# In-place Ln for the last four tiles, a split first load and a new order of the last Exps in a prefix log-sum-exp scan

## Chip, core and metric

The kernel runs on one core of one Trainium2 chip. The metric is the time of one execution on the device in microseconds (us). The kernel before took 1259.39 us, the median of five runs (1258.61 to 1263.86).

## The reference

The input `x` is 8 x 4096 x 2048 in float32. For each of the 8 sequences and each of the 2048 columns the output is the running log-sum-exp along the 4096 time steps:

```
out[:, 0, :] = x[:, 0, :]
mx = maximum(out[:, t-1, :], x[:, t, :])
out[:, t, :] = mx + log(exp(out[:, t-1, :] - mx) + exp(x[:, t, :] - mx))
```

The kernel computes the same quantity as Ln of a prefix sum of Exp. Input and output are 268 MB each, and each is moved once.

## The kernel before

**Tiles.** A tile is 512 time steps of one sequence by all 2048 columns. It lies in SBUF as 128 partitions x 4 rows x 2048 columns: partition p holds the steps 4p to 4p+3. It is 4 MB. There are 64 tiles (`NT`), numbered 0 to 63, eight to a sequence (`NBLK`). Work on a tile is done in two halves of 1024 columns, h = 0 and h = 1.

**Buffers.** Four load buffers `ti` (`NI`), two store buffers `to` (`NO`), two PSUM tiles `ps`. Tile n uses `ti[n % 4]`, `to[n % 2]` and `ps[n % 2]`.

**Steps of a tile**, all ordered by semaphores that are set by hand:

- SP issues the load into `ti` (L111). A load of tile n+4 waits for the `freed` that ScalarE sends when the Ln of tile n is done.
- ScalarE takes Exp in place in `ti`, one instruction for each half (`exp`, L127).
- VectorE adds the four rows up within each partition, three additions of 128 x 1024 for each half (`local`, L232). It takes both halves before it goes on.
- TensorE multiplies the last row by a triangle of ones, which gives every partition the sum of those before it (`triangle`, L208).
- VectorE adds that to all four rows, one 128 x 4096 addition for each half (`join`, L241).
- TensorE carries the tile's last sum over to the next tile's PSUM (`carry`, L197). At the end of a sequence this is only an event. It then raises `carried`.
- ScalarE takes Ln from `ti` into `to`, for each half (`ln`, L132). Half 0 waits until the store before last, which used the same `to`, has landed (`stored`). Each half waits for its `carried`.
- ScalarE waits for both Ln's (`logs`), raises `freed` and issues the store (`store`, L140).

**Order on ScalarE.** Its stream is written out by hand. Two Exps of tile 0 stand first. A loop of 15 turns over four tiles each then has, for n from 1 to 60: Exp of n (both halves), Ln of n-1 (both halves), `freed`, store of n-1. What stands after the loop treats the Exps of tiles 61 to 63 and the Ln's and stores of tiles 60 to 63. For the last pair the order is: Ln of 62 half 0, store of that half, Exp of 63 (both halves), Ln of 62 half 1 and its store, then Ln and store of tile 63 by halves. A step on ScalarE that waits holds up all that stands behind it.

**Queues.** Loads and stores run in two queues, one of SP's and one of ScalarE's, that share the core's 16 DMA engines. The landing of a transfer is complete when all of its engines have reported.

Of the kernel before, what the change touches and what calls it, by code (L numbers as in the profile page):

```python
# [9 lines left out]
def kernel(  # L10
# [2 lines left out]
    x: bass.AP,  # L13
    out: bass.AP,
):

# [13 lines left out]
    ACT = mybir.ActivationFunctionType  # L32
# [46 lines left out]
    with tc.tile_critical():  # L79
        def sems(name, n):  # L80
            return [nc.alloc_semaphore(f"{name}{i}") for i in range(n)]

        ones, shaped, freed, logs = (sems(s, 1)[0] for s in ("ones", "shaped", "freed", "logs"))

        loaded, stored = sems("loaded", NI), sems("stored", NO)
        exps, chain, sums, ahead, joined, carried = (
# [3 lines left out]
        with nc.Block() as block:  # L90

            @block.gpsimd
            def _(g):
                g.memset(before[:], 1.0).then_inc(ones, 1)  # L94
                g.memset(last[:], 1.0).then_inc(ones, 1)  # L95
                g.wait_ge(ones, 2)

                g.affine_select(  # L98
                    out=before[:], in_=before[:], compare_op=mybir.AluOpType.is_ge, fill=0.0,
                    base=-1, pattern=[[1, P]], channel_multiplier=-1,  # L100
                ).then_inc(shaped, 1)

                g.affine_select(  # L103
                    out=last[:], in_=last[:], compare_op=mybir.AluOpType.is_ge, fill=0.0,
                    base=-(P - 1), pattern=[[0, P]], channel_multiplier=1,
                ).then_inc(shaped, 1)

            @block.sync
            def _(sp):
                def load(src, n):  # L110
                    sp.dma_start(out=ti[n][:], in_=src).then_inc(loaded[n], 16)  # L111

                for n in range(NI):
                    load(x_v[n], n)
                with sp.Fori(1, NT // NI) as j:
                    for n in range(NI):
                        sp.wait_ge(freed, n + 1)
                        load(x_v[bass.ds(j * NI + n, 1)][0], n)
                    take(sp, freed, NI)

            @block.scalar
            def _(act):
                def exp(n, h):
                    t = ti[n % NI]
                    if h == 0:
                        take(act, loaded[n % NI], 16)
                    act.activation(t[:, :, half(h)], t[:, :, half(h)], ACT.Exp).then_inc(exps[h], 1)  # L127

                def ln(n, h, turn):
                    if h == 0:  # L130
                        take(act, stored[n % NO], 16)
                    act.activation(  # L132
                        to[n % NO][:, :, half(h)], ti[n % NI][:, :, half(h)], ACT.Ln
                    )._wait_ge(carried[h], turn + 1).then_inc(logs, 1)

                def store(n, dst, h=None, landing=16):
                    t = to[n % NO][:]
                    if h is not None:
                        t, dst = t[:, :, half(h)], dst[:, :, half(h)]
                    act.dma_start(out=dst, in_=t).then_inc(stored[n % NO], landing)  # L140

                def done(turn):

                    event(act, [(logs, 2 * turn + 2)], [(freed, "sem-add-imm", 1)])

                def settle(turns):
                    take(act, carried[0], turns)
                    take(act, carried[1], turns)
                    take(act, logs, 2 * turns)

                for n in range(NO):
                    act.sem_inc(stored[n], 16)
                exp(0, 0)
                exp(0, 1)
                turns = (NT - 2) // NI
                with act.Fori(0, turns) as j:
                    for n in range(1, NI + 1):
                        exp(n, 0)
                        exp(n, 1)
                        ln(n - 1, 0, n - 1)  # L160
                        ln(n - 1, 1, n - 1)
                        done(n - 1)
                        store(n - 1, o_v[bass.ds(j * NI + (n - 1), 1)][0])
                    settle(NI)
                rest = range(1 + turns * NI, NT)
                for turn, n in enumerate(rest):
                    final = n == NT - 1
                    if final:

                        ln(n - 1, 0, turn)  # L170
                        act.wait_ge(logs, 2 * turn + 1)
                        store(n - 1, o_v[n - 1], 0)
                    exp(n, 0)
                    exp(n, 1)
                    if not final:
                        ln(n - 1, 0, turn)
                    ln(n - 1, 1, turn)
                    act.wait_ge(logs, 2 * turn + 2)
                    store(n - 1, o_v[n - 1], 1 if final else None)
                for h in range(2):  # L180
                    ln(NT - 1, h, len(rest))
                    act.wait_ge(logs, 2 * len(rest) + h + 1)
                    store(NT - 1, o_v[NT - 1], h)
                settle(len(rest) + 1)
                for n in (NT - 2, NT - 1):
                    take(act, stored[n % NO], 32)

            @block.tensor
            def _(pe):
                def carry(k, h):  # L190

                    if k == NBLK - 1:
                        event(pe, [(joined[h], k + 1)], [(carried[h], "sem-add-imm", 1)])
                        return
                    for c in range(2 * h, 2 * h + 2):
                        sl = slice(c * FD, (c + 1) * FD)
                        m = pe.matmul(  # L197
                            ps[(k + 1) % 2][:, sl], last[:], ti[k % NI][:, R - 1, sl],
                            start=True, stop=False, skip_group_check=True,
                        )  # L200
                        if c == 2 * h:
                            m._wait_ge(joined[h], k + 1)
                    m.then_inc(carried[h], 1)

                def triangle(k, h):
                    for c in range(2 * h, 2 * h + 2):
                        sl = slice(c * FD, (c + 1) * FD)
                        m = pe.matmul(  # L208
                            ps[k % 2][:, sl], before[:], ti[k % NI][:, R - 1, sl],
                            start=k == 0, stop=True, skip_group_check=True,  # L210
                        )
                        if c == 2 * h:
                            m._wait_ge(sums[h], k + 1)
                    m.then_inc(ahead[h], 1)

                pe.wait_ge(shaped, 2)
                with pe.Fori(0, B):
                    for k in range(NBLK):
                        for h in range(2):
                            triangle(k, h)  # L220
                        for h in range(2):
                            carry(k, h)
                    for h in range(2):
                        take(pe, sums[h], NBLK)
                        take(pe, joined[h], NBLK)

            @block.vector
            def _(dve):
                def local(n, h):
                    t = ti[n]  # L230
                    for r in range(1, R):
                        a = dve.tensor_add(t[:, r, half(h)], t[:, r - 1, half(h)], t[:, r, half(h)])  # L232
                        if r == 1:
                            a._wait_ge(exps[h], n + 1)
                        else:
                            a._wait_ge(chain[h], (R - 2) * n + r - 1)
                        a.then_inc(*((chain[h], 1) if r < R - 1 else (sums[h], 1)))

                def join(n, h):
                    t = ti[n]  # L240
                    dve.tensor_add(  # L241
                        t[:, :, half(h)], t[:, :, half(h)],
                        ps[n % 2][:, half(h)].unsqueeze(1).to_broadcast([P, R, HALF]),
                    )._wait_ge(ahead[h], n + 1).then_inc(joined[h], 1)

                with dve.Fori(0, NT // NI):  # L246
                    for n in range(NI):
                        for h in range(2):
                            local(n, h)
                        for h in range(2):  # L250
                            join(n, h)
                    for h in range(2):
                        take(dve, exps[h], NI)
                        take(dve, chain[h], (R - 2) * NI)
                        take(dve, ahead[h], NI)
# [30 lines left out]
```

The softmax here doesn't subtract the row's maximum and nothing guards it: scores larger than these inputs give would overflow.

## Time and profile before

| what | value |
|---|---|
| median of five runs | 1259.39 us |
| the profiled execution: its time / its span | 1258.78 us / 1257.1 us |
| DMA | 268.44 MB read and 268.44 MB written, mean 427 GB/s over the span |
| VectorE busy | 1023.3 us, 81% |
| ScalarE busy | 913.4 us, 73% |
| TensorE busy | 653.6 us, 52%, mean granted clock 0.783 |
| load, 4096 KB | 64 times, median 31.2 us from issue to landing |
| store, 4096 KB / 2048 KB | 62 / 4 times, median 31.4 / 7.3 us |

Times inside an execution are counted from the start of the span. The span ends some 1.7 us short of the execution's time. Where a row of the profile says "idle before", the engine had nothing to do for so long ahead of that row; the name after the arrow is what ended it. "ACTq L61" means that the engine was held by its own sequencer at a semaphore event, the `take` of line 77, whose instruction is built at line 61.

### The profile page before, as it was taken

To read this page: it belongs to the slowest core of one execution; us is meant where nothing else is said; L and a number is where in the kernel's file an instruction comes from. 1 tells how busy PE (TensorE), PEld (TensorE's weight loads), DVE (VectorE), ACT (ScalarE), POOL (GpSimd) and SP (SyncE) were. 2 spreads that over 40 slices of the span, in tenths; PEclk is the share of its full clock that TensorE was granted. 3 is DMA by queue.
4 is the path that set the end of the run, shared out by engine and by line. 5 is a ranking of instruction groups with operands and counts; after the bars stand their busy time and mean duration, and the time that the engine had idled before them with its cause. 6 is when DMAs were issued, how large, how long until landed. Compare 5 with 4: busy or idle time off the path is not lost. (4 is left out here: it accounts for less than half of the span.)

```text
span 1257.1 us, 3678 instructions
## 1 busy us (share of the span) xinstructions
PE 653.6 (52%) x960; PEld 216.7 (17%) x960; DVE 1023.3 (81%) x512; ACT 913.4 (73%) x257; POOL 1.1 (0%) x8
## 2 busy tenths in 40 slices
PE   2656365553554636555445564555544655455551
PEld 0211121111211211111111111121111211111110
DVE  4999788787887977878778788787887878878865
ACT  5876866777767767677686776866867768677675
POOL 0000000000000000000000000000000000000000
PEclk9897777877778768778687786887768878678776
DMA  9999999999999999999999999999999999999987
GB/s 400 412 433 431 433 432 432 434 431 434 433 434 434 434 434 434 434 433 434 434 434 434 433 434 434 433 433 433 432 433 433 434 433 434 434 433 434 434 381 300
DMA packets 20258, 536.90 MB, mean 427 GB/s; under 512 B 2080, under 2 KB 2080, under 8 KB 4128
## 3 DMA queue, kind: packets, MB, share of 16 engines
q10 hardware_dynamic: 11040, 268.44, 49.6%
q1 hardware_dynamic: 9216, 268.44, 49.6%
q8 instruction: 1, 0.02, 0.0%
q14 instruction: 1, 0.01, 0.0%
HBM read 268.44 MB, written 268.44 MB: 427 GB/s over the span
## 5 line engine op out<-in xcount | busy, mean ns | idle before, releaser
L132 ACT ACTIVATE to<-ti 128x4096 f32<-128x4096 f32 x128 | 456.4, 3609 | 266.9 <-ACTq L61 257.8
L232 DVE TENSOR_TENSOR ti<-ti 128x1024 f32<-128x1024 f32 x384 | 464.6, 1224 | 211.1 <-ACT ti L127 202.3
L241 DVE TENSOR_TENSOR ti<-ti,ps 128x4096 f32<-128x4096 f32 x128 | 560.0, 4417 | 9.8 <-PE ps L208 9.5
L208 PE MATMUL ps<-ti,before 128*128 128x512 f32 x512 | 384.1, 903 | 350.0 <-DVE ti L232 349.2
L127 ACT ACTIVATE ti<-ti 128x4096 f32<-128x4096 f32 x128 | 455.9, 3609 | 66.9 <-ACTq L61 66.9
L197 PE MATMUL ps<-ti,last 128*128 128x512 f32 x448 | 269.5, 732 | 233.9 <-DVE ti L241 233.9
L208 PEld LDWEIGHTS ps<-ti,before 128*128 128x128 f32 x512 | 130.2, 282 | 619.4 <-DVE ti L232 510.8
L197 PEld LDWEIGHTS ps<-ti,last 128*128 128x128 f32 x448 | 86.4, 214 | 400.6 <-DVE ti L241 334.4
L33 ACT ACT_TABLE_LOAD x1 | 1.3, 1283 | 0.8 <-PEq L270 0.8
L98 POOL TENSOR_SCALAR_AFFINE_SELECT before<-before 128x128 f32<-128x128 f32 x1 | 0.3, 295 | 0.1
L103 POOL TENSOR_SCALAR_AFFINE_SELECT last<-last 128x128 f32<-128x128 f32 x1 | 0.3, 295 | 0.0
L95 POOL MEMSET last<- 128x128 f32 x1 | 0.2, 206 | 0.0
L94 POOL MEMSET before<- 128x128 f32 x1 | 0.2, 205 | 0.5 <-SPq L79 0.5
L270 POOL MEMSET const-bfloat16-1.0<- 128x1 bf16 x1 | 0.1, 102 | 0.0
L270 POOL MEMSET const-uint8-127<- 128x1 uint8 x1 | 0.1, 102 | 0.0
L270 POOL MEMSET const-float32-0.0<- 128x1 f32 x1 | 0.1, 99 | 0.3 <-issue 0.3
L270 POOL MEMSET const-float32-1.0<- 128x1 f32 x1 | 0.1, 99 | 0.0
## 6 DMA issues: line engine op xcount, KB each, us to landing
ti<-in_x_dram SPq DMA_DIRECT2D x64, 4096.0 KB, 31.2
out_dram<-to ACTq DMA_DIRECT2D x62, 4096.0 KB, 31.4
out_dram<-to ACTq DMA_DIRECT2D x4, 2048.0 KB, 7.3
```

Source lines behind the costliest of these rows:

```text
L33: nc.scalar.preload_act_table_set("natural_log_exp_and_others")
L94: g.memset(before[:], 1.0).then_inc(ones, 1)
L95: g.memset(last[:], 1.0).then_inc(ones, 1)
L98: g.affine_select(out=before[:], in_=before[:], compare_op=mybir.AluOpType.is_ge, fill=0.0, base=-1, pattern=[[1, P]], channel_multiplier= ...
L103: g.affine_select(out=last[:], in_=last[:], compare_op=mybir.AluOpType.is_ge, fill=0.0, base=-(P - 1), pattern=[[0, P]], channel_multiplier=1,
L127: act.activation(t[:, :, half(h)], t[:, :, half(h)], ACT.Exp).then_inc(exps[h], 1)
L132: act.activation(to[n % NO][:, :, half(h)], ti[n % NI][:, :, half(h)], ACT.Ln)._wait_ge(carried[h], turn + 1).then_inc(logs, 1)
L197: m = pe.matmul(ps[(k + 1) % 2][:, sl], last[:], ti[k % NI][:, R - 1, sl], start=True, stop=False, skip_group_check=True,)
L208: m = pe.matmul(ps[k % 2][:, sl], before[:], ti[k % NI][:, R - 1, sl], start=k == 0, stop=True, skip_group_check=True,)
L232: a = dve.tensor_add(t[:, r, half(h)], t[:, r - 1, half(h)], t[:, r, half(h)])
L241: dve.tensor_add(t[:, :, half(h)], t[:, :, half(h)], ps[n % 2][:, half(h)].unsqueeze(1).to_broadcast([P, R, HALF]),)._wait_ge(ahead[h], n ...
L270: nc = _bacc.Bacc("TRN2", target_bir_lowering=False, num_devices=1)
```

## The change

The change touches the two ends of the program. The loop over the tiles and the instructions of TensorE, VectorE and GpSimd stay as they are.

- **First tile.** Its load is split in two, rows 0 and 1 and rows 2 and 3 of each partition. ScalarE takes Exp of rows 0 and 1 over all columns in one instruction when the first part has landed (`top`), and then Exp of rows 2 and 3 by halves.
- **Last four tiles (60 to 63).** Ln writes in place in `ti`, so it does not wait for a store of `to`. Their stores read `ti` and raise one semaphore of their own (`final`). No load follows into these buffers.
- **Order.** For the last pair the order becomes: Ln of 62 half 0, Exp of 63 half 0, Ln of 62 half 1, store of 62 in one transfer, Exp of 63 half 1, then Ln and store of 63 by halves as before.

```diff
-                for n in range(NI):
+                sp.dma_start(out=ti[0][:, 0:2, :], in_=x_v[0][:, 0:2, :]).then_inc(top, 16)
+                sp.dma_start(out=ti[0][:, 2:R, :], in_=x_v[0][:, 2:R, :]).then_inc(loaded[0], 16)
+                for n in range(1, NI):
                     load(x_v[n], n)
...
-                def ln(n, h, turn):
-                    if h == 0:
+                def ln(n, h, turn, in_place=False):
+                    if h == 0 and not in_place:
                         take(act, stored[n % NO], 16)
                     act.activation(
-                        to[n % NO][:, :, half(h)], ti[n % NI][:, :, half(h)], ACT.Ln
+                        (ti[n % NI] if in_place else to[n % NO])[:, :, half(h)],
+                        ti[n % NI][:, :, half(h)], ACT.Ln,
                     )._wait_ge(carried[h], turn + 1).then_inc(logs, 1)
...
-                exp(0, 0)
-                exp(0, 1)
+                take(act, top, 16)
+                act.activation(ti[0][:, 0:2, :], ti[0][:, 0:2, :], ACT.Exp)
+                exp(0, 0, slice(2, R))
+                exp(0, 1, slice(2, R))
...
-                rest = range(1 + turns * NI, NT)
-                for turn, n in enumerate(rest):
-                    final = n == NT - 1
-                    if final:
-                        ln(n - 1, 0, turn)
-                        act.wait_ge(logs, 2 * turn + 1)
-                        store(n - 1, o_v[n - 1], 0)
-                    exp(n, 0)
-                    exp(n, 1)
-                    if not final:
-                        ln(n - 1, 0, turn)
-                    ln(n - 1, 1, turn)
-                    act.wait_ge(logs, 2 * turn + 2)
-                    store(n - 1, o_v[n - 1], 1 if final else None)
+                for n in range(first + 1, NT):
+                    up = n - 1
+                    if n < NT - 1:
+                        exp(n, 0)
+                        exp(n, 1)
+                        ln(up, 0, up - first, True)
+                        ln(up, 1, up - first, True)
+                        finals += store(up)
+                    else:
+                        ln(up, 0, up - first, True)
+                        exp(n, 0)
+                        ln(up, 1, up - first, True)
+                        finals += store(up)
+                        exp(n, 1)
                 for h in range(2):
-                    ln(NT - 1, h, len(rest))
-                    act.wait_ge(logs, 2 * len(rest) + h + 1)
-                    store(NT - 1, o_v[NT - 1], h)
+                    ln(NT - 1, h, NT - 1 - first, True)
+                    finals += store(NT - 1, h)
```

More of the change, by code (lines that the diff above doesn't have):

```diff
@@ L81, in sems @@
             return [nc.alloc_semaphore(f"{name}{i}") for i in range(n)]
-        ones, shaped, freed, logs = (sems(s, 1)[0] for s in ("ones", "shaped", "freed", "logs"))
+        ones, shaped, freed, logs, top, final = (
+            sems(s, 1)[0] for s in ("ones", "shaped", "freed", "logs", "top", "final")
+        )
         loaded, stored = sems("loaded", NI), sems("stored", NO)
@@ L122, in _, with exp @@
             def _(act):
-                def exp(n, h):
+                def exp(n, h, rows=slice(0, R)):
                     t = ti[n % NI]
@@ L126, in exp @@
                         take(act, loaded[n % NI], 16)
-                    act.activation(t[:, :, half(h)], t[:, :, half(h)], ACT.Exp).then_inc(exps[h], 1)
-                def ln(n, h, turn):
-                    if h == 0:
+                    act.activation(
+                        t[:, rows, half(h)], t[:, rows, half(h)], ACT.Exp
+                    ).then_inc(exps[h], 1)
+                def ln(n, h, turn, in_place=False):
+                    if h == 0 and not in_place:
                         take(act, stored[n % NO], 16)
                     act.activation(
-                        to[n % NO][:, :, half(h)], ti[n % NI][:, :, half(h)], ACT.Ln
+                        (ti[n % NI] if in_place else to[n % NO])[:, :, half(h)],
+                        ti[n % NI][:, :, half(h)], ACT.Ln,
                     )._wait_ge(carried[h], turn + 1).then_inc(logs, 1)
[L136 to L144, printed above, removed]
                 def settle(turns):
@@ L161, in _ @@
                         ln(n - 1, 1, n - 1)
-                        done(n - 1)
-                        store(n - 1, o_v[bass.ds(j * NI + (n - 1), 1)][0])
+                        event(act, [(logs, 2 * n)], [(freed, "sem-add-imm", 1)])
+                        act.dma_start(
+                            out=o_v[bass.ds(j * NI + (n - 1), 1)][0], in_=to[(n - 1) % NO][:]
+                        ).then_inc(stored[(n - 1) % NO], 16)
                     settle(NI)
-                rest = range(1 + turns * NI, NT)
@@ L180, in _, with store @@
-                for h in range(2):
-                    ln(NT - 1, h, len(rest))
-                    act.wait_ge(logs, 2 * len(rest) + h + 1)
-                    store(NT - 1, o_v[NT - 1], h)
-                settle(len(rest) + 1)
-                for n in (NT - 2, NT - 1):
-                    take(act, stored[n % NO], 32)
+                first = turns * NI
+                finals = 0
+                def store(n, h=None):
+                    cols = slice(0, D) if h is None else half(h)
+                    act.wait_ge(logs, 2 * (n - first) + (2 if h is None else h + 1))
+                    act.dma_start(
+                        out=o_v[n][:, :, cols], in_=ti[n % NI][:, :, cols]
+                    ).then_inc(final, 16)
+                    return 1
@@ L188, in _ @@
+                for h in range(2):
+                    ln(NT - 1, h, NT - 1 - first, True)
+                    finals += store(NT - 1, h)
+                settle(NT - first)
+                for n in range(NO):
+                    take(act, stored[n], 16)
+                take(act, final, 16 * finals)
             @block.tensor
```

## The prediction

> **What bounds the kernel now.** I read the slices of the page first, then the DMA share stretch by stretch at both ends, then ScalarE and VectorE in order of time there. The chain that ended last covers only the last 19 us, so it names the end but not its cause. From the page, a slice being 31.4 us:
>
> ```profile
> GB/s 400 412 433 431 433 432 432 434 431 434 433 434 434 434 434 434 434 433 434 434 434 434 433 434 434 433 433 433 432 433 433 434 433 434 434 433 434 434 381 300
> L132 ACT ACTIVATE to<-ti 128x4096 f32<-128x4096 f32 x128 | 456.4, 3609 | 266.9 <-ACTq L61 257.8
> L127 ACT ACTIVATE ti<-ti 128x4096 f32<-128x4096 f32 x128 | 455.9, 3609 | 66.9 <-ACTq L61 66.9
> ```
>
> From the third to the 38th slice the DMA moves 431 to 434 GB/s. ScalarE's 257.8 us of waiting ahead of Ln is a wait for landed stores. So the middle is bound by transfers, and the change doesn't touch it. Only slices 1, 2, 39 and 40 are lower. The stretches there (columns: stretch, length, busy of PE, PEld, DVE, ACT, POOL, clock, DMA share, GB/s):
>
> ```profile
> 13.00:41.00 28.00, 14.64 (x21) 5.13 (x22) 23.54 (x15) 21.48 (x6) 0.00 (x0) 0.94 1.00 431
> 41.00:44.00 3.00, 1.69 (x4) 0.38 (x2) 3.00 (x1) 2.47 (x1) 0.00 (x0) 1.00 0.79 175
> 44.00:64.00 20.00, 12.59 (x20) 4.09 (x20) 19.64 (x10) 18.88 (x7) 0.00 (x0) 0.83 1.01 436
> 1214.00:1218.00 4.00, 3.55 (x4) 1.18 (x4) 4.00 (x2) 3.62 (x2) 0.00 (x0) 0.57 0.14 57
> ```
>
> There is one hole at 41 to 44 us, worth 3 x (434 - 175) / 434 = 1.8 us, and one at 1214 to 1218 us. After the last, compute sets the pace. The first hole is explained by ScalarE's and VectorE's order in time at the start:
>
> ```profile
> 13.32 7.12 ACT L127 ACTIVATE ti<-ti 128x4096 f32<-128x4096 f32 x2 [11.22 <-ACTq L61]
> 37.11 3.62 ACT L132 ACTIVATE to<-ti 128x4096 f32<-128x4096 f32 x1 [2.41 <-PE ps L197]
> 40.99 0.40 ACTq L140 DMA_DIRECT2D out_dram<-to  x1
> ```
> ```profile
> 16.97 7.40 DVE L232 TENSOR_TENSOR ti<-ti 128x1024 f32<-128x1024 f32 x6 [16.97 <-ACT ti L127]
> ```
>
> The first four loads are through at 42.3 (load 0 lands at 13.2, the others each 9.7 later). The next load and the first store are issued only at 41.0, since Ln of tile 0 ends at 40.7. That Ln hangs on carry and join, and so on VectorE, which starts at 16.97 with the first Exp and is busy without a gap over 0.3 us. A load takes some 1.9 us to flow (issue 1.03, landing 12.2 us on, less 9.7 + the last engine's 0.5).
>
> The end, ScalarE and VectorE:
>
> ```profile
> 1171.64 7.12 ACT L132 ACTIVATE to<-ti 128x4096 f32<-128x4096 f32 x2 [4.47 <-ACTq L61]
> 1179.88 7.12 ACT L127 ACTIVATE ti<-ti 128x4096 f32<-128x4096 f32 x2 [1.12 <-ACTq L61]
> 1191.05 7.12 ACT L132 ACTIVATE to<-ti 128x4096 f32<-128x4096 f32 x2 [4.05 <-ACTq L61]
> 1210.50 7.12 ACT L132 ACTIVATE to<-ti 128x4096 f32<-128x4096 f32 x2 [4.67 <-ACTq L61]
> 1220.05 3.62 ACT L132 ACTIVATE to<-ti 128x4096 f32<-128x4096 f32 x1 [2.43 <-ACTq L61]
> 1224.46 7.12 ACT L127 ACTIVATE ti<-ti 128x4096 f32<-128x4096 f32 x2 [0.79 <-ACTq L61]
> ```
> ```profile
> 1190.95 8.75 DVE L241 TENSOR_TENSOR ti<-ti,ps 128x4096 f32<-128x4096 f32 x2
> 1202.35 7.40 DVE L232 TENSOR_TENSOR ti<-ti 128x1024 f32<-128x1024 f32 x6 [2.65 <-ACT ti L127]
> 1228.11 7.40 DVE L232 TENSOR_TENSOR ti<-ti 128x1024 f32<-128x1024 f32 x6 [9.39 <-ACT ti L127]
> 1235.43 8.75 DVE L241 TENSOR_TENSOR ti<-ti,ps 128x4096 f32<-128x4096 f32 x2
> ```
>
> The Ln's are of tiles 59, 60, 61 and 62 (half 0); the Exps of 61 and 63. Ln of 60, 61 and 62 wait 4.05, 4.67 and 2.43 us for stores 58, 59 and 60 to leave `to`. VectorE gets tile 63 only at 1228.11, after 9.39 us idle. From the end of its local sums (1235.5) on, join, Ln, two half stores and landing fill the 21.6 us to 1257.1.
>
> **What the skill says.** "ScalarE: Activation LUTs", What ACT_TABLE_LOAD costs: an ACTIVATE takes 186 ns + 0.833 ns per element, and neighbours overlap by some 93 ns. The trace agrees: 3598 ns by the formula at 4096 elements, 3609 measured, a pair in 7.12 us. "DMA: Bandwidth & Descriptors", Why a DMA increments its semaphore by 16: a DMA's engines finish independently and only the full count is a landing. The trace agrees: store 60, issued at 1198.2, lands 21.7 us later, at 1219.9, though from 1214 nearly all engines are idle (share 0.14). A straggling engine holds Ln of 62. "TensorE: Matmul & The Clock Gate", Part 1: the array runs at half or full clock by its recent activity, in free-running windows of 3.4 us. The trace agrees: a half tile's carry takes 1.98 us in 48 of 56 tiles and up to 3.68 in the other 8 (half 0).
>
> **The change part by part.** All times are on the clock of the execution before.
>
> *First load and Exp.* The two loads take SP one issue more, 0.4 us, hidden by the 9.7 us of queued transfer. Rows 0 and 1 (2 MB, half of 9.7 us) land near 8.4; their Exp (3.6 us) is over by 12.0, before the rest lands at 13.2. Any landing before 9.6 serves. Left after 13.3 is a 2048-element Exp per half, by the skill's formula 1.89 us (an estimate) instead of 3.6. VectorE starts at 15.25 instead of 16.97: 1.7 us earlier. The additional ACTIVATE stands in ScalarE's idle 11.22 us. VectorE passes the 1.7 us on through local, join and carry; Ln half 0 of tile 0 then waits for Exp 1, which ends at 30.14, but half 1 starts 1.7 us earlier (35.4). Load 4 and store 0 go out near 39.3. With 1.9 us to flow that is 41.2, before the queue runs dry, and the hole closes. Everything behind is paced by transfers and moves with it. Bounds: 0, if the hole is the price of starting the first store; 1.7 at most, by VectorE. The issue alone (41.0 + 1.9 = 42.9, against engines free from 41.8) explains 1.1. I take **1.5**.
>
> *In-place Ln.* Same shape and engine as the Exp in place, 3609 ns as Ln before: no cost. Bounds are nothing and the few ns between the two rows. Ln of 60 needs carry 60, over by 1183.7, so it follows Exp 61 at once: 1187.0 to 1194.1, 4.05 earlier. Store 60 and Exp 62 (load 62 landed at 1190.7) follow at 1194.7. VectorE takes local 62 right behind join 61, 1199.7 to 1207.1, 2.65 earlier; join 62 half 0 ends at 1211.7 (with 0.2 for the triangle), its carry at 1213.8. Ln of 61 runs 1201.8 to 1209.0, so store 61 is issued before store 60 is out and the hole at 1214 closes. But transfers don't set the end here, so that is worth nothing by itself. What is late next is carry 62: Ln of 62 half 0 starts at 1213.8 instead of 1220.05.
>
> *Order.* From 1213.8: Ln half 0, Exp 63 half 0, Ln half 1 (its carry is over by 1219.9 at worst, needed at 1220.9), each 3.56, to 1224.5. The store's issue, 0.35, and events 0.14, hold the second Exp until 1225.0; it ends at 1228.6. VectorE has added half 0 meanwhile, and takes half 1 in 3.7 us, to 1232.4 instead of 1235.5. So Exp 63 half 1 pays for the Ln put ahead of it, and of the 6.2 us gained at Ln 62, **3.1** remain. Join, Ln and the two half stores follow as before. Store 62, now one 4 MB transfer behind store 61, is out at about 1219.9 + 2 x 9.7 = 1239.3 on the slowest engine, ahead of store 63's first half at 1240.5. Had carry 62 half 0 run at half clock, Ln 62 starts 1.7 later and 1.4 remain. The final waits take one event more, under 0.1.
>
> Sum: 1.5 + 3.1 = 4.6 us off the profiled execution's 1258.78 (span 1257.1 and 1.7 around it), 1254.2. That execution lies 0.6 below the median, so against the median it is **1254.8**.
>
> **Rivals.**
> - *Carry 62 at half clock.* The triangles and carries of tile 62 move closer to those of 61, which could change the windows either way; 8 of 56 speak for one in seven, and this execution had 3.68 right at tile 62. Gain 1.5 + 1.4 = 2.9: 1256.5. Chance 0.17.
> - *The hole at 41 us stays*, because the first store must start beside a load whenever it comes. Store and load both showed a start-up of some 1 to 2 us at other places, but there the queues were empty. Gain 3.1 at the tail alone: 1256.3. Chance 0.13.
> - *The split load doesn't split*: both parts share the engines and land together at 13.2. Then three Exps follow, and VectorE starts 1.75 later than before. Gain 3.1 - 1.75 = 1.4: 1258.0. Against it: queued loads 0 to 3 landed 9.7 apart, in turn. Chance 0.04.
> - *Slower: stores alone drain too slowly.* Stores 61 and 62 now queue without loads between. At r GB/s they end at 1219.9 + 8389/r; from below 392 GB/s they delay store 63, and below 317 (end after 1246.4) both gains are gone. At 300 the end is 1247.9, and the time 1.5 above the median, 1260.9. Against it: store 60 alone took 9.5 us (1210.4 to 1219.9), 442 GB/s. Chance 0.03.
>
> **How the numbers follow.** The forecast has 0.63, the rivals the rest. A measurement tells about 0.3% from no change, 3.8 us here. The forecast's own span, with the head between 1.1 and 1.7, is a gain of 4.2 to 4.8, beyond that bound by little, and the medians scatter by some 0.7; so 0.55 of its 0.63 count as faster, and 0.02 of the first two rivals: 0.57. Slower 0.04, the rest 0.39 within. The range: 1253.2 (the forecast's best and the scatter) to 1258.0 (the split that fails, or both first rivals at once).
>
> **What would show it.** Right: VectorE's first addition near 15.3; the second load into the first buffer issued near 39.3; no stretch under 400 GB/s at 41 to 44; no wait ahead of Ln 60 and 61; from VectorE's last local addition to the end 21.6 us, as before. Wrong: a first addition at 18.7, a first store that starts with the same hole, a 3.7 us carry ahead of Ln 62, or last half stores that take over 7 us to land. A gain above 5.5 us or a loss would say that the ends are not what moved.

## The result, and the profile after

The changed kernel takes 1254.23 us, the median of 30 runs (1253.36 to 1276.9), against 1259.19 us for the kernel before (51 runs). The ratio is 0.9963, with a 95% interval of 0.9952 to 0.9975; it is formed over the runs, without the slow one at 1276.9 us, and is not the quotient of the medians (0.9961). The medians lie 4.96 us apart; the forecast was 4.6 us and 1254.8 us. The profiled execution took 1255.20 us, with a span of 1253.5 us, so it is 1.0 us above its median.

In the changed file the Exps stand at L133 (the first one at L153), Ln at L140, the loop's store at L165, the last stores at L177, the local sums at L248, the join at L257 and the carry at L213.

The start, ScalarE's order in time and then VectorE's:

```profile
8.47 3.62 ACT L153 ACTIVATE ti<-ti 128x4096 f32<-128x4096 f32 x1 [6.38 <-ACTq L62]
13.35 3.71 ACT L133 ACTIVATE ti<-ti 128x2048 f32<-128x2048 f32 x2 [1.27 <-ACTq L62]
...
34.26 3.62 ACT L140 ACTIVATE to<-ti 128x4096 f32<-128x4096 f32 x1 [0.56 <-PE ps L213]
38.14 0.41 ACTq L165 DMA_DIRECT2D out_dram<-to  x1
```
```profile
15.30 7.39 DVE L248 TENSOR_TENSOR ti<-ti 128x1024 f32<-128x1024 f32 x6 [15.30 <-ACT ti L133]
```

The first half of the load has landed at 8.4, its Exp is over before the rest lands, and what is left are two short Exps (3.71 us for both, where the two long ones took 7.12). VectorE starts at 15.30 instead of 16.97. The first store goes out at 38.1 instead of 41.0. The transfers beside it (columns as before, GB/s last):

```profile
41.00:44.00 3.00, 0.74 (x2) 0.30 (x2) 3.00 (x2) 3.00 (x2) 0.00 (x0) 1.00 0.76 295
44.00:64.00 20.00, 10.75 (x21) 3.27 (x19) 19.86 (x10) 16.12 (x6) 0.00 (x0) 0.91 0.99 418
1214.00:1218.00 4.00, 1.98 (x4) 0.68 (x4) 1.63 (x1) 4.00 (x2) 0.00 (x0) 1.00 1.03 442
```

The hole at 1214 is gone (442 GB/s, before 57). The hole at 41 is smaller (295, before 175) but has not closed, and the stretch behind it moves 418 GB/s instead of 436: together the two lose 1.7 us, as they did before. The view counts a packet where it starts; with each packet spread over its own time the loss from 36 to 66 us is 1.3 us in this execution and 1.8 us in the one before. The end, ScalarE and then VectorE:

```profile
1171.36 7.12 ACT L140 ACTIVATE to<-ti 128x4096 f32<-128x4096 f32 x2 [4.48 <-ACTq L62]
...
1179.60 7.12 ACT L133 ACTIVATE ti<-ti 128x4096 f32<-128x4096 f32 x2 [1.12 <-ACTq L62]
1186.63 7.11 ACT L140 ACTIVATE ti<-ti 128x4096 f32<-128x4096 f32 x2
...
1201.29 7.11 ACT L140 ACTIVATE ti<-ti 128x4096 f32<-128x4096 f32 x2
...
1213.37 3.62 ACT L140 ACTIVATE ti<-ti 128x4096 f32<-128x4096 f32 x1 [4.97 <-PE ps L213]
1216.89 3.60 ACT L133 ACTIVATE ti<-ti 128x4096 f32<-128x4096 f32 x1
1220.40 3.60 ACT L140 ACTIVATE ti<-ti 128x4096 f32<-128x4096 f32 x1
...
1224.42 3.62 ACT L133 ACTIVATE ti<-ti 128x4096 f32<-128x4096 f32 x1 [0.42 <-ACT ti L140]
```
```profile
1199.27 7.39 DVE L248 TENSOR_TENSOR ti<-ti 128x1024 f32<-128x1024 f32 x6
...
1220.53 3.74 DVE L248 TENSOR_TENSOR ti<-ti 128x1024 f32<-128x1024 f32 x3 [4.90 <-ACT ti L133]
1228.07 3.74 DVE L248 TENSOR_TENSOR ti<-ti 128x1024 f32<-128x1024 f32 x3 [3.79 <-ACT ti L133]
1231.73 8.74 DVE L257 TENSOR_TENSOR ti<-ti,ps 128x4096 f32<-128x4096 f32 x2
```

Ln of 60 and 61 have no wait ahead of them. What is late next is the carry of tile 62 (4.97 us, released by PE). Ln of 62 half 0 starts at 1213.37, before 1220.05. But VectorE now waits twice for tile 63, 4.90 and 3.79 us: the second wait is the Ln and the store that the order puts ahead of the second Exp. From VectorE's last join (1231.73) to the end are 21.7 us (21.6 before).

**A mark to compare ends by.** In both kernels ScalarE's work at the end starts from the landing of store 57 (1171.5 before, 1171.2 after: issue and 31.4 us). From there to the end of the span are 85.5 us before and 82.2 us after. (The kernel before also waits for the stores behind it, up to store 60, which landed 48.4 us after store 57.) So in these two executions the end gives 3.3 us and the head 0.3 us. The landing itself moves from one execution to the next, which the experiments below had to separate.

### The profile page after: what moved, and what is told of

The parts are those of the page before. It is cut to its first block, busy times and chain, and to the rows that moved or that the text cites. A ratio compares the mean times of both kernels' runs of the same rounds, so it can differ in the third digit from the quotient of the medians.

```text
span 1253.5 us, 3677 instructions
## 1 busy us (share of the span) xinstructions
PE 653.5 (52%) x960; PEld 215.5 (17%) x960; DVE 1022.9 (82%) x512; ACT 913.3 (73%) x258; POOL 1.1 (0%) x8
## 5 line engine op out<-in xcount | busy, mean ns | idle before, releaser
L248 DVE TENSOR_TENSOR ti<-ti 128x1024 f32<-128x1024 f32 x384 | 464.7, 1224 | 208.2 <-ACT ti L133 199.5
L140 ACT ACTIVATE to<-ti 128x4096 f32<-128x4096 f32 x120 | 427.7, 3609 | 249.9 <-ACTq L62 248.7
L257 DVE TENSOR_TENSOR ti<-ti,ps 128x4096 f32<-128x4096 f32 x128 | 560.0, 4416 | 9.4 <-PE ps L224 8.9
L133 ACT ACTIVATE ti<-ti 128x4096 f32<-128x4096 f32 (+1 forms) x128 | 452.6, 3582 | 59.8 <-ACTq L62 59.4
L213 PE MATMUL ps<-ti,last 128*128 128x512 f32 x448 | 272.7, 740 | 231.1 <-DVE ti L257 231.1
L213 PEld LDWEIGHTS ps<-ti,last 128*128 128x128 f32 x448 | 86.2, 213 | 400.4 <-DVE ti L257 334.1
L140 ACT ACTIVATE ti<-ti 128x4096 f32<-128x4096 f32 x8 | 28.7, 3606 | 13.9 <-PEq L62 8.9
L153 ACT ACTIVATE ti<-ti 128x4096 f32<-128x4096 f32 x1 | 3.6, 3616 | 6.4 <-ACTq L62 6.4
```

Source lines behind the costliest of these rows:

```text
L133: act.activation(t[:, rows, half(h)], t[:, rows, half(h)], ACT.Exp).then_inc(exps[h], 1)
L140: act.activation((ti[n % NI] if in_place else to[n % NO])[:, :, half(h)], ti[n % NI][:, :, half(h)], ACT.Ln,)._wait_ge(carried[h], turn + ...
L153: act.activation(ti[0][:, 0:2, :], ti[0][:, 0:2, :], ACT.Exp)
L213: m = pe.matmul(ps[(k + 1) % 2][:, sl], last[:], ti[k % NI][:, R - 1, sl], start=True, stop=False, skip_group_check=True,)
L257: dve.tensor_add(t[:, :, half(h)], t[:, :, half(h)], ps[n % 2][:, half(h)].unsqueeze(1).to_broadcast([P, R, HALF]),)._wait_ge(ahead[h], n ...
```

## The experiments

Each is timed beside the kernel before on the same chip. That kernel's medians were 1259.11 us (experiments 1 to 4), 1259.27 us (5 to 7) and 1259.28 us (8). "Less" and "more" are differences of medians.

**1. The head alone.** The first load and Exp of the change, the end of the kernel before.

```diff
-                for n in range(NI):
+                sp.dma_start(out=ti[0][:, 0:2, :], in_=x_v[0][:, 0:2, :]).then_inc(top, 16)
+                sp.dma_start(out=ti[0][:, 2:R, :], in_=x_v[0][:, 2:R, :]).then_inc(loaded[0], 16)
+                for n in range(1, NI):
                     load(x_v[n], n)
...
+                take(act, top, 16)
+                act.activation(ti[0][:, 0:2, :], ti[0][:, 0:2, :], ACT.Exp)
+                exp(0, 0, slice(2, R))
+                exp(0, 1, slice(2, R))
```

> The kernel before with the split first load and the split Exp of tile 0 alone. Theory S (my sum): VectorE starts 1.7 us earlier, load 4 and store 0 are issued at about 38 to 39 us instead of 41.0, the hole at 41 to 44 us closes, and the time falls by 1.1 to 1.7 us, to about 1257.6. Rival H (the hole is the price of the first store, whenever it comes): the issue is as early, but the first landing of the second load stays at 63.6 us and the time falls by 0.5 us at most, to 1258.7 to 1259.2.

Measured: 1258.53 us, 0.6 less than before, ratio 0.9996 (0.9974 to 1.0018). Its profiled execution was a late one (1262.26 us; store 57 lands at 1175.4), and the interval takes in both theories. The first store went out at 39.24 us. The kernel was run again in experiment 8.

**2. The end alone.** The change with the old load and Exp of tile 0.

```diff
-                sp.dma_start(out=ti[0][:, 0:2, :], in_=x_v[0][:, 0:2, :]).then_inc(top, 16)
-                sp.dma_start(out=ti[0][:, 2:R, :], in_=x_v[0][:, 2:R, :]).then_inc(loaded[0], 16)
-                for n in range(1, NI):
+                for n in range(NI):
                     load(x_v[n], n)
...
-                take(act, top, 16)
-                act.activation(ti[0][:, 0:2, :], ti[0][:, 0:2, :], ACT.Exp)
-                exp(0, 0, slice(2, R))
-                exp(0, 1, slice(2, R))
+                exp(0, 0)
+                exp(0, 1)
```

> The change without its head: in-place Ln and the new order at the end, load and Exp of tile 0 as before. Theory S: 3.1 us less, about 1256.1, with Ln of 62 half 0 some 6.2 us and VectorE's last local sums some 3.1 us earlier than before. Rival H, by which the head is worth nothing and all of the 4.96 us between the medians comes from the end: 4.5 to 5 us less, 1254.2 to 1254.7.

Measured: 1255.72 us, 3.4 less, ratio 0.9969 (0.9954 to 0.9983). Store 57 lands at 1171.7 and the span ends 82.2 us later, as in the change. The interval alone, 2.1 to 5.8 us, would take in the rival's 4.5 to 5 us too; against it stand the span, which is 3.3 us shorter from the landing on, and the second measurement in experiment 8 (3.3 less). So the end is worth 3.3 to 3.4 us and not the whole gain.

**3. In-place Ln with the old order** (with the old head, as in experiment 2; the diff is against the change).

```diff
...
                     else:
                         ln(up, 0, up - first, True)
+                        finals += store(up, 0)
                         exp(n, 0)
-                        ln(up, 1, up - first, True)
-                        finals += store(up)
                         exp(n, 1)
+                        ln(up, 1, up - first, True)
+                        finals += store(up, 1)
```

> In-place Ln of the last four tiles alone, with the order of before at the end (Ln 62 half 0, its half store, both Exps of 63, Ln 62 half 1, its half store), and the head of before. Theory S (the sum's step on the order): Ln of 62 half 0 starts 6.2 us earlier as in the change, both Exps follow at once, VectorE has the last local sums at 1229.2 instead of 1235.5; the gain is 6.2 us, or some 5.8 if the last stores then queue behind those before (slowest engine free at 1239.5): 1253.0 to 1253.5, faster than the in-place Ln with the new order by some 2.7 to 3.1 us. Rival: in-place Ln and the new order only gain together (the order is what lets tile 63 start early): in place alone gains under 2 us, 1257.5 or more.

Measured: 1254.56 us, 4.55 less, ratio 0.9968 (0.9948 to 0.9988); the runs lie widely apart, from 1251.8 up. In the profiled execution (1251.80 us) the span ends 79.4 us after store 57, 6.1 less than before. VectorE has tile 63's sums in one piece:

```profile
1220.80 7.40 DVE L245 TENSOR_TENSOR ti<-ti 128x1024 f32<-128x1024 f32 x6 [5.81 <-ACT ti L131]
1228.41 8.75 DVE L254 TENSOR_TENSOR ti<-ti,ps 128x4096 f32<-128x4096 f32 x2 [0.22 <-PE ps L221]
```

The join starts 3.3 us earlier than in the change, 2.7 us when both are counted from store 57. The median of 4.55 lies between the theories, and its interval (1.5 to 6.5 us) takes in both; the profile agrees with mine, and experiment 7 decides.

**4. The new order alone** (Ln into `to`, with its waits, and the old head).

```diff
-                    if final:
-                        ln(n - 1, 0, turn)
-                        act.wait_ge(logs, 2 * turn + 1)
-                        store(n - 1, o_v[n - 1], 0)
-                    exp(n, 0)
-                    exp(n, 1)
...
+                    else:
+                        ln(n - 1, 0, turn)
+                        exp(n, 0)
+                        ln(n - 1, 1, turn)
+                        act.wait_ge(logs, 2 * turn + 2)
+                        store(n - 1, o_v[n - 1])
+                        exp(n, 1)
```

> The new order of the last pair alone: Ln 62 half 0, Exp 63 half 0, Ln 62 half 1, store 62 in one, Exp 63 half 1; Ln writes into the store buffers as before and waits for their stores; head of before. Theory S: Ln of 62 half 0 still waits for store 60 (1220.05), the second Exp of 63 ends some 3.1 us later than before, 1234.8, and the time rises by about 3 us, to 1262.3. Rival: the order gains by itself, since VectorE gets the first half of 63 at 1227.2 instead of 1228.1: time unchanged or up to 1 us less.

Measured: 1262.05 us, 2.9 more, ratio 1.0021 (1.0010 to 1.0033). The profiled execution was a late one (1264.98 us), so times are counted from the start of Ln of 62. ScalarE and VectorE show why:

```profile
1223.18 3.62 ACT L132 ACTIVATE to<-ti 128x4096 f32<-128x4096 f32 x1 [2.57 <-ACTq L61]
```
```profile
1230.34 3.75 DVE L233 TENSOR_TENSOR ti<-ti 128x1024 f32<-128x1024 f32 x3 [7.56 <-ACT ti L127]
1237.88 3.74 DVE L233 TENSOR_TENSOR ti<-ti 128x1024 f32<-128x1024 f32 x3 [3.79 <-ACT ti L127]
```

VectorE gets the first half of tile 63 7.2 us after Ln of 62 starts, against 8.1 us before (1220.05 to 1228.11): the order gains 0.9 us here. But the second half waits 3.79 us more, and the sums of tile 63 end 18.4 us after that start instead of 15.5. The order by itself makes the kernel slower by 2.9 us.

**5. Both Exps of 63 ahead of Ln of 62** (the change otherwise).

```diff
-                    if n < NT - 1:
-                        exp(n, 0)
-                        exp(n, 1)
-                        ln(up, 0, up - first, True)
-                        ln(up, 1, up - first, True)
-                        finals += store(up)
-                    else:
-                        ln(up, 0, up - first, True)
-                        exp(n, 0)
-                        ln(up, 1, up - first, True)
-                        finals += store(up)
-                        exp(n, 1)
+                    exp(n, 0)
+                    exp(n, 1)
+                    ln(up, 0, up - first, True)
+                    ln(up, 1, up - first, True)
+                    finals += store(up)
```

> The change with both Exps of tile 63 ahead of both Ln's of tile 62 (load 63 has landed at 1210.0, and ScalarE is idle from 1208.8 to 1213.4 in the change). Theory (the order costs time, ScalarE's place for Exp 63 is the idle stretch): VectorE gets tile 63 right behind join 62, last local sums at about 1223 instead of 1231.8, store 63 half 0 issued at about 1231; then the end is set by the queue of stores, slowest engine through with store 62 at 1239.1 and with 63 at 1249.3, span 1250.8: about 2.7 us under the change, 1251.5. Rival: the end of the change already hangs on the stores' slowest engine, not on ScalarE's order: within 0.7 us of the change, 1253.5 to 1255.

Measured: 1251.29 us, ratio to before 0.9927 (0.9907 to 0.9947), and 3.15 us under the change on the same chip; its slowest run (1251.59) is below the fastest of the change (1253.21). ScalarE and VectorE:

```profile
1208.78 7.13 ACT L133 ACTIVATE ti<-ti 128x4096 f32<-128x4096 f32 x2 [1.66 <-ACTq L62]
1215.81 7.11 ACT L140 ACTIVATE ti<-ti 128x4096 f32<-128x4096 f32 x2
...
1229.71 0.62 ACTq L177 DMA_DIRECT2D out_dram<-ti  x1
```
```profile
1214.21 7.39 DVE L241 TENSOR_TENSOR ti<-ti 128x1024 f32<-128x1024 f32 x6
1221.52 8.74 DVE L250 TENSOR_TENSOR ti<-ti,ps 128x4096 f32<-128x4096 f32 x2
```

The Exps stand in ScalarE's idle stretch, and VectorE goes from join 62 into tile 63 with no wait. The last join starts 8.9 us earlier than in the change, counted from store 57 in both, and yet the kernel is only 3.15 us faster: the first half store is issued at 1229.7, but store 62 lands on its slowest engine at 1237.9, and the two halves behind it at 1242.8 and 1247.7. The end is now set by the queue of stores. This version beats both kernels.

**6. The change again, and with an early small store.** The change itself ran beside experiment 5 and this one. The edit stores 128 rows of 512 bytes of a constant into a part of the output that the last stores overwrite:

```diff
+                act.wait_ge(shaped, 2)
+                act.dma_start(out=o_v[NT - 1][:, 0, 0:P], in_=last[:]).then_inc(warm, 16)
                 take(act, top, 16)
...
+                take(act, warm, 16)
                 turns = (NT - 2) // NI
```

The change: 

> The change itself once more, on the chip of its neighbours. Theory D (the head is worth under 1 us, half the hole being the price of the first store; the end is worth 3.1 to 3.4): 4 to 4.3 us less than before. Rival S (head 1.5 as in my sum): 4.6 to 5 us less. In its profile by theory D the transfers lost between 40 and 48 us are again 0.9 us against 1.8 before.

With the small store: 

> The change with a small store (128 rows of 512 bytes of a constant into the last tile's part of the output, which the last stores overwrite) issued by ScalarE before its first Exp, while the first loads run; ScalarE waits for it ahead of the loop. It tells what the rest of the hole is. Theory F (the first use of the store queue or of the output costs it): the rest of 0.9 us shrinks to 0.3 or less, no slow load packets (2.5 us instead of 1.2) near 40 us, and the time falls by some 0.6 us against the change. Theory B (starting stores beside running loads costs it, first or not): the loss at 40 to 48 us stays at 0.8 to 1.0 us and the time is that of the change.

Measured: the change 1254.44 us (4.8 less than before, ratio 0.9956, 0.9937 to 0.9976), with the small store 1255.19 us (0.9961, 0.9948 to 0.9974). Its profile is 1.0 us longer than the change's from store 57 on, 0.6 us of it a longer wait for the carry of tile 62. The stretch from 40 to 48 us, in this order: before, the change (its first profile), the change again, with the small store:

```profile
40.00:48.00 8.00, 3.97 (x8) 1.36 (x8) 8.00 (x3) 7.19 (x3) 0.00 (x0) 1.00 0.90 328
```
```profile
40.00:48.00 8.00, 3.40 (x9) 1.02 (x7) 8.00 (x3) 8.00 (x3) 0.00 (x0) 1.00 1.01 389
```
```profile
40.00:48.00 8.00, 4.57 (x8) 1.39 (x7) 8.00 (x3) 6.64 (x3) 0.00 (x0) 0.79 1.00 393
```
```profile
40.00:48.00 8.00, 4.75 (x8) 1.24 (x6) 8.00 (x3) 6.43 (x3) 0.00 (x0) 0.79 1.00 389
```

Lost against 434 GB/s are 8 x (434 - 328) / 434 = 2.0 us before, and 0.8 us in the three others. The small store had landed at 11.9 and changed nothing at 40 us. So the rest is not the first use of the queue or of the output (theory F falls). It lies where the stream of stores starts beside running loads. Which start causes it is not shown: the second load into the first buffer is issued at the same moment as the first store in every run. The packets tell the two parts of the hole apart. Between 39 and 48 us the engines of the kernel before stand idle for 0.6 us on the mean, and 16 load packets that take 2.4 us on the mean, where the others take 1.21, add 1.2 us. In the change no engine is idle, and the slow packets (1.9 us on the mean) add 0.9 us. The time of the change agrees with the larger size of the head (theory S), while its hole is that of theory D.

**7. The change with the old order** (the edit of experiment 3 made to the change).

> The change with the order of before in the last pair (Ln 62 half 0, half store, both Exps of 63, Ln 62 half 1, half store): in-place Ln and the split first load without the new order. Theory (the order gives back some 3 us of what in-place Ln gains, less what the queue of stores then takes): VectorE's last local sums at about 1228.5, span 1250 to 1251.5, 1.5 to 3 us under the change. Rival (the in-place kernel without the head gained 4.55 in the median against 3.4 with the new order, and that 1.1 us is all): 0.7 to 1.3 under the change.

Measured: 1251.69 us, ratio to before 0.9930 (0.9910 to 0.9951), 2.75 us under the change on the same chip. The span ends 79.4 us after store 57 (the change: 82.2 in the profile beside it). The runs lie within 0.6 us, and all of them below the fastest run of the change. With experiment 4 this settles the order: it costs 2.8 to 2.9 us with in-place Ln and without. Experiment 5 is only 0.4 us faster than this kernel.

**8. The head's worth beside three ends.** The change without its head (experiment 2), the change, the head alone (experiment 1) and experiment 5 with the old head, on one chip.

Without the head: 

> The change without its head, on one chip with the change, the head alone and a third end, so that the head's worth is read beside each end. Both theories: 3.2 to 3.5 us under the kernel before, which has the same head.

The change: 

> The change. Theory Q (the head is worth what the hole at 40 to 48 us shrinks by, 1.8 to 0.9, whatever the end): 0.9 us or less under the change without its head. Theory L (an earlier first store also lets the stores run ahead of the loads on some engines; the end of the change hangs on store 57, the end of before on store 60, at which no load is left to be ahead of): 1.3 to 1.5 us under it.

The head alone: 

> The split first load and Exp alone. Theories Q and L: 0.6 to 0.9 us under the kernel before, since its end hangs on store 60 and on the hole alone. My sum: 1.5 us under.

Exps first, old head: 

> In-place Ln with both Exps of 63 ahead of both Ln's of 62, first load and Exp in one as before. Its end hangs on the whole queue of stores. Theories Q and L: the head's 0.9 us over the same end with the split load (1251.3): 1252.2. If the head is worth nothing where the end is set by transfers: 1251.3.

Measured:

| kernel | median us | ratio to before (95%) | first store issued | lost 40 to 48 us | store 57 / store 60 landed |
|---|---|---|---|---|---|
| change without its head | 1255.97 | 0.9973 (0.9962 to 0.9985) | 40.9 | 2.1 | 1171.5 / 1220.0 |
| change | 1253.28 | 0.9943 (0.9929 to 0.9958) | 38.2 | 0.9 | 1170.3 / 1218.8 |
| head alone | 1258.07 | 0.9990 (0.9977 to 1.0004) | 38.6 | 0.8 | 1170.0 / 1218.5 |
| Exps first, old head | 1252.62 | 0.9949 (0.9930 to 0.9969) | 39.9 | 1.4 | 1173.7 / 1219.9 |

The head is worth 1.2 us alone (its interval reaches past 1, so no change is not excluded), 1.3 us beside the end of experiment 5 (1251.29, another chip) and 2.7 us between the first two rows, of 22 and 6 runs, whose best runs lie 1.55 apart. For this pair theory Q allowed 0.9 us and theory L 1.5. The hole shrinks by 1.2 us from the kernel before (2.0) to the head alone, by 1.2 us between the first two rows, and by 0.6 us from the last row to experiment 5 (389 GB/s, 0.8). So beside the end of before the hole accounts for the gain, beside that of experiment 5 for about half of it.

What the hole hangs on is the moment of the first store, and not the split load as such. Experiment 3 has the old head, but in its profile the carry of tile 0 half 1 ran at full clock (1.98 us, before 3.68), and the store went out 1.7 us earlier:

```profile
39.31 0.41 ACTq L161 DMA_DIRECT2D out_dram<-to  x1
```
```profile
40.00:48.00 8.00, 4.94 (x8) 1.50 (x8) 8.00 (x3) 6.97 (x2) 0.00 (x0) 0.86 1.01 389
```

Over all 14 profiles the loss from 40 to 48 us is 2.0 to 2.1 us with the first store at 40.9 to 41.1 us (three profiles), 1.4 to 1.5 us at 39.9 (two), and 0.8 to 0.9 us from 39.3 down to 37.6 (nine). With packets spread over their time it is 1.8 to 1.9, 1.7, and 0.7 to 1.0 us.

Theory L holds in some executions. In the change's first profile and both of experiment 6, the median engine has reported store 57 at 1164.6 to 1165.0 us, and load 61, issued beside it, only at 1167.1 to 1167.3; in the kernel before the two come at 1167.2 and 1167.0. So there the stores had run ahead of the loads. In the profile of the change in the table they had not (1166.2 and 1166.3). ScalarE waits for the last engine: that one had gained 2.2 us in the change's profile of experiment 6 (1169.3), but only 0.3 us in the first (1171.2). That such executions make up the rest of the 2.7 us is not shown; four of the second row's six runs lie at 1253.2 to 1253.3 us, as that profile of experiment 6 does (1253.21).

The profile of the change in this group happens to show what the first rival described, here ScalarE and then TensorE:

```profile
1214.10 3.62 ACT L140 ACTIVATE ti<-ti 128x4096 f32<-128x4096 f32 x1 [6.63 <-PE ps L213]
```
```profile
1210.38 3.68 PE L213 MATMUL ps<-ti,last 128*128 128x512 f32 x4 [2.35 <-DVE ti L257]
1214.72 1.98 PE L213 MATMUL ps<-ti,last 128*128 128x512 f32 x4 [0.65 <-DVE ti L257]
```

The carry of 62 half 0 ran at half clock (3.68 us; 1.98 in the first profile of the change), Ln waited 6.63 us, the span ended 83.9 us after store 57 instead of 82.2, and this execution took 1255.90 us, the slowest of its six.

## Why the prediction was right, and where it was not

- **The sum.** 4.6 us forecast, 4.96 measured. Both terms were of the right size: the end 3.1 against 3.3 to 3.4 (experiment 2 and the span after store 57), the head 1.5 against 1.2 to 1.5, the latter between the medians of the change (1254.23) and of experiment 2 (1255.72), with a wider reading of 2.7 on one chip.
- **In-place Ln.** Right. The Ln's cost 3606 ns in place and 3609 ns as before; Ln of 62 half 0 starts 42.1 us after store 57 has landed, where the sum had 42.3.
- **The order.** The step that took 6.2 us down to 3.1 is right: 2.9 us lost by the order alone, 2.75 us won by undoing it. The prediction counted the cost, but did not say that without this part the change would gain more.
- **The head.** VectorE's start was right (15.30, sum 15.25). The first store went out 1.2 us earlier than the sum had it, because the carry of tile 0 half 1 took 2.50 us and not 3.68: Ln half 1 starts at 34.26, not at 35.4. That was chance, and it brought nothing: the head alone had its store at 39.24 in experiment 1, as in the sum, and lost the same 0.8 us. What failed is the step "the hole closes": 0.8 to 0.9 us of the loss stay in every profile with the new head, though stores are issued as early as 37.6. The rival that the hole stays had half of it. The size came out partly by luck. The hole gave up about what the issue alone explained (1.2 against 1.1), and the estimate lay little above that; but by the same sum a store issued at 39.9 (41.8 with its 1.9 us to flow) would have closed it, and the two profiles with such a store still lost 1.4 to 1.5 us.
- **Carry at half clock.** Of six profiles with this end one shows it in full, at the price given (1.7 us), and the one with the small store in part (a wait of 5.56 us).
- **The split that fails** did not happen: the first part landed at 8.4.
- **Stores that drain too slowly** did not happen: stores 60, 61 and 62 land at 1219.7, 1229.5 and 1239.1, so 61 and 62 took 9.7 us each or some 432 GB/s; the sum had 1239.3. The rival's limit of 392 GB/s does not follow from its own figures: 8389 / (1240.5 - 1219.9) is 407.
- **The marks.** Right were the first addition, no wait ahead of Ln 60 and 61, and the 21.6 us behind VectorE's last local addition (21.7). The second load into the first buffer went out with the store, at 38.1 instead of 39.3, and 41 to 44 us stayed under 400 GB/s. Two marks of being wrong tell nothing. The last half store took 7.8 us to land (1244.24 to 1252.05), over the 7 us named, but also 7.7 us in the kernel before (1247.95 to 1255.66). And a gain above 5.5 us was to say that the ends are not what moved; in experiment 8 the change gained 6.0 us by its median, while its profile shows the same two ends.

## What to carry to other kernels

Where an engine's stream is written by hand, put an instruction into the stretch in which that engine waits, not ahead of the one that the next engine is waiting for. In-place Ln alone made 6.1 us in the profile, and the new order of four instructions gave 2.8 to 2.9 of them back. The two Exps moved into a 5 us idle stretch won 3.15 us on top of the change, of which the old order would have won 2.75.

When the middle of a kernel is bound by transfers, compare the ends from a landing that both kernels share, since the landing itself moves by more between executions (1169.3 to 1175.6 us for store 57) than the change is worth. An end freed of one wait runs into the next one: here the carry, then the queue of stores.

## What the runs showed of the hardware

- When the first large store starts beside running loads, some 16 to 20 of the loads' 32 KB packets, about one on each engine, take longer than the usual 1.21 us: 2.4 us on the mean in the kernel before, 1.9 us in the change. The store's first packet moves only 3.4 to 5.0 us after its issue. An earlier small store does not change it (1.9 and 4.5 us). Whether the store or the load issued with it slows the packets is not shown.
- Some of the 16 DMA engines fall behind. In the kernel before, first and last engine report a store 0.8 us apart at 63 us and 4.7 us apart at 1171 us, where one engine is 3.3 us behind all others. How far they fall behind differs: store 57 landed between 1169.3 and 1175.6 us in the profiles of this study. Two executions of the head alone, on two chips, that lie 4.6 us apart (1257.62 and 1262.26 us) had it at 1170.0 and 1175.4.
